# A SwiGLU FFN inside a two-block model: gate and up by seven half products, the FFN in two phases

## The chip, the cores and the metric

The kernel runs on one core of one Trainium2 chip. Its engines are TensorE (PE in the rows; PEld is its weight load), VectorE (DVE), ScalarE (ACT), GpSimd (POOL) and SyncE (SP), which here issues the DMAs. The metric is the device time of one execution in microseconds: 2137.47 us for the kernel before, the median of 3 runs (2134.62 to 2138.95).

## The reference

Two model blocks on 1024 tokens of width 1024, all in f32. The first has four mixers (mLSTM, a spatial gating unit, a convolution, S5), an output projection, a layer norm, and then the part that is changed here:

```python
x = layer_norm(ALPHA * x + g1 * y, ln1_w, ln1_b)
x = layer_norm(ALPHA * x + g2 * swiglu(x * (1.0 + sc2) + sh2, w_ffn_in, w_ffn_out), ln2_w, ln2_b)

def swiglu(h, w_in, w_out):
    g, u = split(h @ w_in, 2)            # w_in: 1024 x 5632
    return (silu(g) * u) @ w_out         # w_out: 2816 x 1024
```

The second block (retention, sparse attention, a gated embedding) starts on the result tile by tile.

## The kernel before

All data lie in pages of 128 x 1024 f32. Every f32 product is made of three matmuls of a fast f32 type: an operand is split into hi (ScalarE copies and rounds, L173) and lo (VectorE subtracts, L174), and hi x hi, lo x hi and hi x lo are added up in PSUM (L184 to L186, or L195 to L197 where the loop yields between them). A page pool (46 pages), a pool of 3 raw buffers for what is loaded and split, and PSUM in two pools of 4 banks (mm and ax) set when a load or a product may begin.

The FFN has 22 slices j of 128 of its 2816 columns. The layer-normed tokens, transposed, scaled and split (L334 to L341), lie in two halves of 512 tokens, hh and hl. For each slice and half, `Ffn.half` (L350) makes gate and up with 8 k x 3 matmuls of 512 columns each, then silu (ScalarE, L366), the product (VectorE, L367) and its split ah, al (L368, L369). `stage_b` (L372) goes over the slices in blocks of two: behind the four halves of a block it loads two slices of w_ffn_out, POOL multiplies them by the modulation row g2 (L412), they are split, and `item` (L429) makes the down product for each of the 8 token tiles, two column halves each, which VectorE adds to the tile's residual acc (L436). The last block's items go on to the second layer norm and into the second model block, in a pipe with that block's work.

The residual acc of the 8 tiles stays on chip from the first layer norm on. `residual` scales it in the first FFN block: two rows are scaled on POOL (L383), and each tile is multiplied (VectorE, L386) and added to (POOL, L387). Weights of the second model block are split beside the FFN and put by in DRAM ("spare", PS steps a block).

Each engine takes its instructions in the order in which the program records them, so the position of an operation in these loops sets what it is queued behind.

Of the kernel before, what the change touches and what calls it, by code (L numbers as in the profile page):

```python
# [255 lines left out]
class Front:  # L256


    def __init__(self, k, y_s, mod_s, x, wo, w_fi, have):
# [15 lines left out]
    def items(self):  # L275
# [9 lines left out]
        self.ffn = Ffn(self.k, self.hT, self.w_fi)  # L285
        yield self.ffn.half(0, 0, GS)

    def tile_in(self, t):
# [35 lines left out]
        s1, t1 = self.s1, self.t1
        for i in range(8):
# [4 lines left out]
            hi, lo = ph[0][:, i % 2], ph[1][:, i % 2]  # L330
            self.hT[t // 4].append((hi, lo))
            pt = k.ax.tile([128, 512], F32, name="ax")
            for j in range(4):
                nc.tensor.transpose(pt[:, j * 128:j * 128 + 128], self.acc[t // 4 * 4 + j][:, i * 128:i * 128 + 128], k.ident)  # L334
# [1 line left out]
            ht = page("htmp", shape=[128, 512])
            if i in HTA:
                nc.scalar.activation(ht, pt, AF.Identity, scale=s1[:, i:i + 1], bias=t1[:, i:i + 1])
            else:
                nc.vector.tensor_scalar(ht, pt, s1[:, i:i + 1], t1[:, i:i + 1], op0=ALU.mult, op1=ALU.add)  # L340
            (nc.vector if i % 2 else nc.gpsimd).tensor_tensor(lo, ht, hi, op=ALU.subtract)  # L341


class Ffn:


    def __init__(self, k, hT, w_fi):
        self.k, self.hT, self.w_fi, self.w, self.a = k, hT, w_fi, {}, {}

    def half(self, j, half, c=8):  # L350
        k, nc, page = self.k, self.k.nc, self.k.page
        if j not in self.w:
            self.w[j] = [k.wload(dap(self.w_fi, (i * (DFF // 128) + j) * 131072, [[1024, 128], [128, 8], [1, 128]]), [128, 8, 128])
                         for i in range(2)]
            self.a[j] = page("ah", dt=F32R), page("al", dt=F32R)
        (wg, wu), (ah, al) = self.w[j], self.a[j]
        hs = slice(half * 512, half * 512 + 512)
# [1998 lines left out]
```

## Time and profile before

| | |
|---|---|
| time, median of 3 runs | 2137.47 us (2134.62 to 2138.95) |
| profiled execution, its own time | 2141.31 us |
| its span, first to last instruction | 2139.5 us |
| mean granted TensorE clock | 0.971 of full speed |
| busy: TensorE, VectorE, ScalarE, POOL | 94%, 60%, 37%, 20% |
| FFN, first gate product to last down product | about 614 to 1340 us |
| HBM traffic over the span | 139 GB/s |

A row of a group of instructions has the line, the engine, the operation with output and inputs, the shape, the count, and then the busy time in us, the mean of one in ns, and the idle time just before them with what ended it. In a timeline a row starts with the start and the duration in us; the idle time before it stands in brackets. Matmuls overlap, so their pace is read from their starts.

### The profile page before, as it was taken

What the parts mean: (1) busy time and instruction counts of PE and PEld (TensorE: products, weight loads), DVE (VectorE), ACT (ScalarE), POOL (GpSimd) and SP (SyncE); (2) the same over time, 40 slices, a digit from 0 to 9 for tenths busy, and PEclk for the clock granted to TensorE, in tenths of its full rate; (3) what the DMA queues carried; (4) which work ended last, traced back from release to release, by engine and by line L of the source; (5) the groups of instructions that cost most, each with busy time, mean ns of one, the idle gap of its engine ahead of it and who ended that gap; (6) DMA issues with size and microseconds to landing.
All of it is one profiled execution on the core that took longest, in us unless ns stands there. A gap on an engine that the chain in (4) does not pass through costs nothing. (4 is left out here: it accounts for less than half of the span.)

```text
span 2139.5 us, 29059 instructions
## 1 busy us (share of the span) xinstructions
PE 2019.0 (94%) x10808; PEld 1673.6 (78%) x10808; DVE 1281.4 (60%) x2620; ACT 785.4 (37%) x1568; POOL 429.0 (20%) x465
## 2 busy tenths in 40 slices
PE   8897898999998999999999999899999998899998
PEld 3787897877877888888887788786787886688886
DVE  6967636476686334554446543857788746856533
ACT  2521134343131222222222221545787524355432
POOL 1454403112144000000000000441002221200032
PEclk9999898989999999999999999999999998999999
DMA  8465564456411335554345534313312205343611
GB/s 291 158 157 139 141 204 139 166 173 225 172 47 61 106 111 201 187 206 147 130 157 187 206 133 147 138 40 109 148 50 89 89 24 163 128 154 120 226 60 69
DMA packets 144334, 299.32 MB, mean 140 GB/s; under 512 B 30648, under 2 KB 70072, under 8 KB 144192
## 3 DMA queue, kind: packets, MB, share of 16 engines
q1 hardware_dynamic: 144192, 297.46, 41.5%
q8 instruction: 85, 1.39, 0.3%
q14 instruction: 57, 0.47, 0.1%
HBM read 208.81 MB, written 87.56 MB: 139 GB/s over the span
## 5 line engine op out<-in xcount | busy, mean ns | idle before, releaser
L195 PE MATMUL mm<-hh,whi 128*128 128x512 f32 x704 | 275.2, 391 | 4.4 <-ACT whi L173 4.4
L197 PE MATMUL mm<-hh,wlo 128*128 128x512 f32 x704 | 275.1, 391 | 1.4 <-DVE wlo L174 1.4
L196 PE MATMUL mm<-hl,whi 128*128 128x512 f32 x704 | 274.8, 390 | 0.0
L184 PE MATMUL mm<-whi,xTh 128*128 128x512 f32 (+1 forms) x576 | 227.8, 399 | 3.9 <-DMA whi<-scr_wsp 2.6
L185 PE MATMUL mm<-wlo,xTh 128*128 128x512 f32 (+1 forms) x576 | 225.2, 392 | 2.5 <-DMA wlo<-scr_wsp 2.5
L186 PE MATMUL mm<-whi,xTl 128*128 128x512 f32 (+1 forms) x576 | 223.7, 391 | 0.0
L174 DVE TENSOR_TENSOR wlo<-raw,whi 128x1024 fp32r<-128x1024 f32 (+2 forms) x99 | 126.0, 1293 | 129.4 <-ACT whi L173 128.7
L412 POOL TENSOR_TENSOR raw<-raw,g2b 128x1024 f32<-128x1024 f32 x22 | 54.1, 2463 | 597.2 <-DMA raw<-in_w_ffn_out 569.6
L195 PEld LDWEIGHTS mm<-hh,whi 128*128 128x128 f32 x704 | 132.5, 188 | 32.4 <-ACT whi L173 5.3
L197 PEld LDWEIGHTS mm<-hh,wlo 128*128 128x128 f32 x704 | 132.5, 188 | 30.0 <-DVE wlo L174 2.7
L184 PE MATMUL mm<-whi,hhi 128*128 128x256 f32 (+1 forms) x512 | 152.0, 297 | 3.3 <-DVE csg L1526 1.7
L196 PEld LDWEIGHTS mm<-hl,whi 128*128 128x128 f32 x704 | 132.6, 188 | 27.5
L186 PE MATMUL mm<-whi,hlo 128*128 128x256 f32 (+1 forms) x512 | 149.6, 293 | 1.9 <-POOL hlo L1370 1.5
L185 PE MATMUL mm<-wlo,hhi 128*128 128x256 f32 (+1 forms) x512 | 150.5, 294 | 0.0
L184 PE MATMUL ax<-whi,ah 128*128 128x512 f32 x352 | 139.1, 397 | 8.9 <-ACT whi L173 5.7
L173 ACT ACTIVATE whi<-raw 128x1024 fp32r<-128x1024 f32 (+2 forms) x99 | 100.9, 1047 | 125.7 <-DMA raw<-in_w_fi_o 68.3
L436 DVE TENSOR_TENSOR acc<-ax,acc 128x512 f32<-128x512 f32 x176 | 116.5, 684 | 41.0 <-PE ax L186 40.7
L185 PE MATMUL ax<-wlo,ah 128*128 128x512 f32 x352 | 138.8, 394 | 0.2 <-DVE wlo L174 0.2
L186 PE MATMUL ax<-whi,al 128*128 128x512 f32 x352 | 138.3, 393 | 0.0
L367 DVE TENSOR_TENSOR sg<-mm,sg 128x512 f32<-128x512 f32 x44 | 30.4, 690 | 168.0 <-PE mm L197 157.7
L184 PEld LDWEIGHTS mm<-whi,xTh 128*128 128x128 f32 x576 | 109.3, 190 | 26.4 <-DMA whi<-scr_wsp 4.5
L185 PEld LDWEIGHTS mm<-wlo,xTh 128*128 128x128 f32 x576 | 109.3, 190 | 22.5 <-DMA wlo<-scr_wsp 3.6
(616 smaller groups left out, 4477.6 us busy)
## 6 DMA issues: line engine op xcount, KB each, us to landing
raw<-in_w_fi_o SPq DMA_DIRECT2D x44, 512.0 KB
wmr<-in_w_mod SPq DMA_DIRECT2D x32, 512.0 KB
raw<-in_w_in_2o SPq DMA_DIRECT2D x24, 512.0 KB
scr_wsp<-phi SPq DMA_DIRECT2D x24, 512.0 KB
scr_wsp<-plo SPq DMA_DIRECT2D x24, 512.0 KB
whi<-scr_wsp SPq DMA_DIRECT2D x24, 512.0 KB
wlo<-scr_wsp SPq DMA_DIRECT2D x24, 512.0 KB
raw<-in_w_ffn_out SPq DMA_DIRECT2D x22, 512.0 KB
```

The lines of the kernel that those rows point to most:

```text
L173: nc.scalar.activation(hi, raw, AF.Copy)
L174: nc.vector.tensor_tensor(lo, raw, hi, op=ALU.subtract)
L184: nc.tensor.matmul(ps, ah, bh, start=k == 0, stop=False)
L185: nc.tensor.matmul(ps, ah, bl, start=False, stop=False)
L186: nc.tensor.matmul(ps, al, bh, start=False, stop=k == n - 1)
L195: nc.tensor.matmul(ps, ah, bh, start=k == 0, stop=False)
L196: nc.tensor.matmul(ps, ah, bl, start=False, stop=False)
L197: nc.tensor.matmul(ps, al, bh, start=False, stop=k == n - 1)
L367: nc.vector.tensor_tensor(sg, pu, sg, op=ALU.mult)
L412: nc.gpsimd.tensor_tensor(raw, raw, g2b, op=ALU.mult)
L436: nc.vector.tensor_tensor(v[:, cs], ps, v[:, cs], op=ALU.add)
```

## The change

Gate and up of one slice are together a product of a 2 x 2 block matrix of weights (gate and up by two halves of k) with a 2 x 2 block matrix of tokens (two halves of k by two halves of tokens). The change makes it with Strassen's scheme (seven block products and sums of blocks instead of eight products): each of the seven has 4 k x 3 matmuls of 512 columns, 84 a slice. The tokens' sums t1 to t4 are made once (`high_half`); each slice's sums of weights are made in `load`, four of them on POOL, and all seven operands are split; the sums of products are made on VectorE as the products leave PSUM (`one`, `two`, `three`, `four`).

The FFN then runs in two phases, since the token operands fill the pages: phase 1 makes the activations of all 22 slices and stores each to DRAM (`scr_act`); the residual is stored to DRAM too (`scr_res`), when it is made. Phase 2 is the down product, in a block of 2 and five of 4 slices: the activation is loaded again and split, w_ffn_out is multiplied and split as before, and the items of the first block load the residual, multiply it (VectorE) and add to it (POOL). The steps for the second model block's weights are dealt out anew over both phases.

```diff
+        nc.sync.dma_start(dap(self.res, t * 131072, [[1024, 128], [1, 1024]]), v)
...
+    def high_half(self):
+        k, nc, page, s1, t1, hf, B = self.k, self.k.nc, self.k.page, self.s1, self.t1, self.hf, self.B
+        fs = []
+        def split(n, i, x):
+            if i % 2 == 0:
+                self.sp = [page(f"{n}{c}{i}", F32R, [128, 2, 512]) for c in "hl"]
+            hi, lo = self.sp[0][:, i % 2], self.sp[1][:, i % 2]
+            nc.scalar.activation(hi, x, AF.Copy)
+            nc.vector.tensor_tensor(lo, x, hi, op=ALU.subtract)
+            B[n].append((hi, lo))
+        for i in range(4):
+            if i:
+                yield 1
+            f = page(f"hg{i}", shape=[128, 2, 512])
+            fs.append(f)
+            nc.vector.tensor_scalar(f[:, 0], self.turned(1, i), s1[:, i:i + 1], t1[:, i:i + 1], op0=ALU.mult, op1=ALU.add)
+            nc.scalar.activation(f[:, 1], self.turned(1, i + 4), AF.Identity, scale=s1[:, i + 4:i + 5], bias=t1[:, i + 4:i + 5])
+            nc.vector.tensor_tensor(hf[i], f[:, 0], hf[i], op=ALU.subtract)
+            split('t1', i, hf[i])
+        for i in range(4):
+            yield 1
+            nc.gpsimd.tensor_tensor(hf[i], fs[i][:, 1], hf[i], op=ALU.subtract)
+            split('t2', i, hf[i])
+        for i in range(4):
+            nc.gpsimd.tensor_tensor(hf[i + 4], hf[i + 4], hf[i], op=ALU.subtract)
+            split('t4', i, hf[i + 4])
+        for i in range(4):
+            yield 1
+            split('22', i, fs[i][:, 1])
+        for i in range(4):
+            yield 1
+            nc.gpsimd.tensor_tensor(fs[i][:, 0], fs[i][:, 1], fs[i][:, 0], op=ALU.subtract)
+            split('t3', i, fs[i][:, 0])
+        hf.clear()
...
+    def load(self, j):
+        k, nc = self.k, self.k.nc
+        raw = []
+        for i in range(2):
+            r = k.raw([128, 8, 128])
+            nc.sync.dma_start(r, dap(self.w_fi, (i * (DFF // 128) + j) * 131072, [[1024, 128], [128, 8], [1, 128]]))
+            raw.append(r)
+        (a11, a12), (a21, a22) = [(r[:, 0:4], r[:, 4:8]) for r in raw]
+        self.w[j] = w = {}
+        def split(n, x):
+            p = k.wpage("fw", shape=[128, 2, 4, 128])
+            k.split(p[:, 0], p[:, 1], x)
+            w[n] = p[:, 0], p[:, 1]
+        split('11', a11)
+        split('12', a12)
+        yield 1
+        sp = k.page("fsa", shape=[128, 2, 4, 128])
+        sq = k.page("fsb", shape=[128, 2, 4, 128])
+        nc.gpsimd.tensor_tensor(sp[:, 0], a21, a22, op=ALU.add)
+        nc.gpsimd.tensor_tensor(sp[:, 1], sp[:, 0], a11, op=ALU.subtract)
+        split('s1', sp[:, 0])
+        split('s2', sp[:, 1])
+        yield 1
+        nc.gpsimd.tensor_tensor(sq[:, 0], a12, sp[:, 1], op=ALU.subtract)
+        nc.gpsimd.tensor_tensor(sq[:, 1], a11, a21, op=ALU.subtract)
+        split('s4', sq[:, 0])
+        yield 1
+        split('s3', sq[:, 1])
+        split('22', a22)
...
+    def one(self, j):
+        k, nc = self.k, self.k.nc
+        self.o[j] = e, u = [k.page(n, shape=[128, 2, 512]) for n in ("fe", "fu")]
+        nc.scalar.activation(e[:, 1], self.prod(j, '11', '11', k.mm), AF.Copy)
+        yield 1
+        nc.vector.tensor_tensor(e[:, 0], self.prod(j, '12', '21', k.mm), e[:, 1], op=ALU.add)
+        nc.scalar.activation(e[:, 0], e[:, 0], AF.Silu)
+    def two(self, j):
+        k, nc = self.k, self.k.nc
+        e, u = self.o[j]
+        nc.vector.tensor_tensor(u[:, 0], self.prod(j, 's2', 't2', k.ax), e[:, 1], op=ALU.add)
+        yield 1
+        nc.vector.tensor_tensor(u[:, 1], self.prod(j, 's1', 't1', k.ax), u[:, 0], op=ALU.add)
+    def three(self, j):
+        k, nc = self.k, self.k.nc
+        e, u = self.o[j]
+        nc.vector.tensor_tensor(e[:, 1], self.prod(j, 's4', '22', k.ax), u[:, 1], op=ALU.add)
+        nc.scalar.activation(e[:, 1], e[:, 1], AF.Silu)
+        yield 1
+        ps = self.prod(j, 's3', 't3', k.ax)
+        nc.vector.tensor_tensor(u[:, 1], ps, u[:, 1], op=ALU.add)
+        nc.vector.tensor_tensor(u[:, 0], ps, u[:, 0], op=ALU.add)
+        nc.vector.tensor_tensor(e[:, 1], u[:, 1], e[:, 1], op=ALU.mult)
+    def four(self, j):
+        k, nc = self.k, self.k.nc
+        e, u = self.o.pop(j)
+        nc.vector.tensor_tensor(u[:, 0], self.prod(j, '22', 't4', k.mm), u[:, 0], op=ALU.add)
+        nc.vector.tensor_tensor(e[:, 0], u[:, 0], e[:, 0], op=ALU.mult)
+        nc.sync.dma_start(dap(self.act, j * 131072, [[1024, 128], [1, 1024]]), e.rearrange("p a b -> p (a b)"))
+        del self.w[j]
...
+    def rest(self):
+        n = DFF // 128
+        ld = self.ld[2]
+        for j in range(n):
+            for _ in self.two(j):
+                next(ld, None)
+            yield j
+            if j:
+                self.four(j - 1)
+            next(ld, None)
+            for _ in self.three(j):
+                next(ld, None)
+            for _ in ld:
+                pass
+            ld = self.load(j + 3) if j + 3 < n else iter(())
+            next(ld, None)
+            if j + 2 < n:
+                for _ in self.one(j + 2):
+                    pass
+        self.four(n - 1)
...
+    for j in front.ffn.rest():
+        if j >= 2:
+            for _ in range(1 + j % 2):
+                next(spare, None)
+    front.B.clear()
+    g2b, aw, ab = page("g2b"), page("aw"), page("ab")
+    k.bcast(g2b, mod_s, 5120, 1024)
+    for p, w in ((aw, ln1_w), (ab, ln1_b)):
+        k.bcast(p, w, 0, 1024)
+        nc.gpsimd.tensor_scalar(p, p, ALPHA, None, op0=ALU.mult)
+    blocks = [range(2)] + [range(j, j + 4) for j in range(2, NF, 4)]
+    for n, blk in enumerate(blocks):
+        last = n == len(blocks) - 1
+        acts, wf = [], []
+            acts.append(k.wload(dap(act, j * 131072, [[1024, 128], [1, 1024]]), [128, 1024]))
             raw = k.raw()
             nc.sync.dma_start(raw, dap(w_fo, j * 131072, [[1024, 128], [1, 1024]]))
             nc.gpsimd.tensor_tensor(raw, raw, g2b, op=ALU.mult)
             hl = page("whi", F32R), page("wlo", F32R)
             k.split(*hl, raw)
             wf.append(hl)
...
+            if n == 0:
+                acc[t] = page(f"acc{t}")
+                nc.sync.dma_start(acc[t], dap(res, t * 131072, [[1024, 128], [1, 1024]]))
+                nc.vector.tensor_tensor(acc[t], acc[t], aw, op=ALU.mult)
+                nc.gpsimd.tensor_tensor(acc[t], acc[t], ab, op=ALU.add)
```

On POOL at the start of the FFN there stood before the last subtractions of the token halves, the scaling of two rows, and eight residual additions, of which the first two are shown, ahead of the multiplication of w_ffn_out (numbers behind names are buffers):

```order
L341 TENSOR_TENSOR hl0_5860<-htmp_5867,hh0_5859 128x512
L341 TENSOR_TENSOR hl2_5892<-htmp_5899,hh2_5891 128x512
L341 TENSOR_TENSOR hl4_5925<-htmp_5932,hh4_5924 128x512
L341 TENSOR_TENSOR hl6_5957<-htmp_5964,hh6_5956 128x512
L383 TENSOR_SCALAR aw_5995<-aw_5995 128x1024
L383 TENSOR_SCALAR ab_5996<-ab_5996 128x1024
L387 TENSOR_TENSOR acc0_5499<-acc0_5499,ab_5996 128x1024
L387 TENSOR_TENSOR acc1_5316<-acc1_5316,ab_5996 128x1024
```

Now four subtractions (`L354`) are followed by 20 additions and subtractions of 512 columns. Shown are the last twelve: hg are tokens' sums t3, hf those of t2 (L382) and t4 (L385), fsa and fsb sums of weights:

```order
L382 TENSOR_TENSOR hf0_5736<-hg1_5919,hf0_5736 128x512
L385 TENSOR_TENSOR hf4_5821<-hf4_5821,hf0_5736 128x512
L392 TENSOR_TENSOR hg2_5972<-hg2_5972 128x512
L425 TENSOR_TENSOR fsa_6021<-raw_5777 128x512
L382 TENSOR_TENSOR hf2_5787<-hg2_5972,hf2_5787 128x512
L426 TENSOR_TENSOR fsa_6021<-fsa_6021,raw_5775 128x512
L385 TENSOR_TENSOR hf6_5853<-hf6_5853,hf2_5787 128x512
L430 TENSOR_TENSOR fsb_6022<-raw_5775,fsa_6021 128x512
L431 TENSOR_TENSOR fsb_6022<-raw_5775,raw_5777 128x512
L392 TENSOR_TENSOR hg3_6005<-hg3_6005 128x512
L382 TENSOR_TENSOR hf2_5787<-hg3_6005,hf2_5787 128x512
L385 TENSOR_TENSOR hf6_5853<-hf6_5853,hf2_5787 128x512
```

The residual's work has left this place; tokens' sums and weights' sums stand mixed, and the last one of t2 (`hf2_5787<-hg3_6005`) is the nineteenth of the twenty. On TensorE the first product behind the turned tiles is the one that reads t2:

```order
L335 MATMUL ax_6012<-ident_73,acc4_5031 128x128
L335 MATMUL ax_6012<-ident_73,acc5_5231 128x128
L335 MATMUL ax_6012<-ident_73,acc6_5409 128x128
L335 MATMUL ax_6012<-ident_73,acc7_5606 128x128
L184 MATMUL ax_6104<-t2h0_6043,fw_5942 128x512
L184 MATMUL ax_6128<-t1h0_5900,fw_5939 128x512
L185 MATMUL ax_6104<-t2l0_6044,fw_5942 128x512
L186 MATMUL ax_6104<-t2h0_6043,fw_5942 128x512
```

Every product stands behind this one on TensorE, where before the next products needed the token halves alone.

Where phase 1 now ends, SP's queue has this (before, the loads of a block stood among those of the next products' weights, with no store of an activation and no load of acc):

```order
L479 DMA scr_act_102<-fe_8920 128x1024
L155 DMA g2b_9290<-scr_mod_90 128x1024
L155 DMA aw_9291<-in_ln1_w 128x1024
L155 DMA ab_9292<-in_ln1_b 128x1024
L539 DMA raw_9304<-in_w_ffn_out 128x1024
L160 DMA raw_9311<-scr_act_102 128x1024
L479 DMA scr_act_102<-fe_9067 128x1024
L539 DMA raw_9317<-in_w_ffn_out 128x1024
L160 DMA raw_9484<-scr_act_102 128x1024
L539 DMA raw_9490<-in_w_ffn_out 128x1024
L563 DMA acc0_9324<-scr_res_103 128x1024
L563 DMA acc1_9344<-scr_res_103 128x1024
```

The store of the last activation (`fe_9067`) stands ahead of the second slice of w_ffn_out and of the eight loads of acc. POOL had at such a place only multiplications by g2b, four rows for two blocks after the last residual addition:

```order
L387 TENSOR_TENSOR acc7_5599<-acc7_5599,ab_5996 128x1024
L412 TENSOR_TENSOR raw_6198<-raw_6198,g2b_6196 128x1024
L412 TENSOR_TENSOR raw_6205<-raw_6205,g2b_6196 128x1024
L412 TENSOR_TENSOR raw_6588<-raw_6588,g2b_6196 128x1024
L412 TENSOR_TENSOR raw_6595<-raw_6595,g2b_6196 128x1024
```

Now it has there:

```order
L540 TENSOR_TENSOR raw_9490<-raw_9490,g2b_9290 128x1024
L565 TENSOR_TENSOR acc0_9324<-acc0_9324,ab_9292 128x1024
L565 TENSOR_TENSOR acc1_9344<-acc1_9344,ab_9292 128x1024
L565 TENSOR_TENSOR acc2_9364<-acc2_9364,ab_9292 128x1024
L565 TENSOR_TENSOR acc3_9384<-acc3_9384,ab_9292 128x1024
L565 TENSOR_TENSOR acc4_9404<-acc4_9404,ab_9292 128x1024
L565 TENSOR_TENSOR acc5_9424<-acc5_9424,ab_9292 128x1024
L565 TENSOR_TENSOR acc6_9444<-acc6_9444,ab_9292 128x1024
L565 TENSOR_TENSOR acc7_9464<-acc7_9464,ab_9292 128x1024
L540 TENSOR_TENSOR raw_9503<-raw_9503,g2b_9290 128x1024
L540 TENSOR_TENSOR raw_9516<-raw_9516,g2b_9290 128x1024
L540 TENSOR_TENSOR raw_9529<-raw_9529,g2b_9290 128x1024
```

The residual additions, eight in a row, have moved from the FFN's first block to this place, behind the first multiplication for block 1 and ahead of the other three.

## Rows read from the trace of the kernel before

**Rows 1.** The page: busy us, share of the span and instructions of each engine.

```profile
PE 2019.0 (94%) x10808; PEld 1673.6 (78%) x10808; DVE 1281.4 (60%) x2620; ACT 785.4 (37%) x1568; POOL 429.0 (20%) x465
```

**Rows 2.** The page's costliest group: busy us, mean ns, idle before.

```profile
L195 PE MATMUL mm<-hh,whi 128*128 128x512 f32 x704 | 275.2, 391 | 4.4 <-ACT whi L173 4.4
```

**Rows 3.** Timeline of TensorE: start, duration, in brackets the idle time before.

```profile
639.83 0.39 PE L196 MATMUL mm<-hl,whi 128*128 128x512 f32 x1
...
661.59 0.39 PE L196 MATMUL mm<-hl,whi 128*128 128x512 f32 x1
...
667.87 0.79 PE L184 MATMUL ax<-whi,ah 128*128 128x512 f32 x1 [5.67 <-ACT whi L173]
```

**Rows 4.** Windows: length, then busy of PE, PEld, DVE, ACT, POOL, clock, DMA, GB/s.

```profile
664.00:668.00 4.00, 0.13 (x1) 0.13 (x1) 0.15 (x1) 1.06 (x1) 4.00 (x3) 0.94 0.00 0
668.00:672.00 4.00, 3.77 (x8) 2.52 (x9) 4.00 (x4) 2.52 (x3) 1.04 (x1) 0.50 0.23 53
672.00:676.00 4.00, 4.00 (x14) 3.17 (x13) 2.90 (x5) 0.43 (x1) 0.00 (x0) 0.71 0.80 241
...
900.00:950.00 50.00, 50.00 (x222) 41.42 (x221) 24.84 (x32) 14.64 (x22) 3.21 (x2) 1.00 0.40 141
1150.00:1200.00 50.00, 46.10 (x195) 37.40 (x194) 21.67 (x30) 12.03 (x16) 4.79 (x2) 0.97 0.24 75
1200.00:1250.00 50.00, 48.41 (x212) 39.45 (x211) 26.09 (x31) 11.60 (x13) 4.80 (x2) 1.00 0.60 217
1350.00:1400.00 50.00, 43.92 (x202) 37.83 (x203) 34.73 (x88) 23.53 (x51) 21.16 (x31) 0.93 0.39 149
...
1380.00:1385.00 5.00, 2.39 (x7) 1.50 (x8) 2.90 (x19) 2.14 (x8) 2.05 (x7) 0.93 1.03 414
```

**Rows 5.** Timelines of VectorE (two rows), then of POOL.

```profile
618.81 0.81 DVE L320 TENSOR_SCALAR acc<-acc,rs_r,ln_nm 128x1024 f32<-128x1024 f32 x1
...
643.13 1.21 DVE L386 TENSOR_TENSOR acc<-acc,aw 128x1024 f32<-128x1024 f32 x1
...
621.87 3.00 POOL L341 TENSOR_TENSOR hl<-htmp,hh 128x512 fp32r<-128x512 f32 x2 [3.11 <-DVE htmp L340]
...
629.32 2.79 POOL L383 TENSOR_SCALAR aw<-aw 128x1024 f32<-128x1024 f32 x1
...
648.42 16.01 POOL L387 TENSOR_TENSOR acc<-acc,ab 128x1024 f32<-128x1024 f32 x5 [1.23 <-DVE acc L386]
664.40 4.65 POOL L412 TENSOR_TENSOR raw<-raw,g2b 128x1024 f32<-128x1024 f32 x2
...
716.34 2.39 POOL L412 TENSOR_TENSOR raw<-raw,g2b 128x1024 f32<-128x1024 f32 x1 [29.94 <-DMA raw<-in_w_ffn_out]
```

**Rows 6.** Line L341, one subtraction of 512 columns: ns min/median/max by engine.

```profile
L341 POOL TENSOR_TENSOR hl<-htmp,hh x8: 1282/1298/1974, 607.2 to 627.9; 128x512 fp32r<-128x512 f32 x8
L341 DVE TENSOR_TENSOR hl<-htmp,hh x8: 672/692/1483, 608.4 to 629.4; 128x512 fp32r<-128x512 f32 x8
```

**Rows 7.** Groups of the FFN's stretch: busy us, mean ns, idle before.

```profile
L436 DVE TENSOR_TENSOR acc<-ax,acc 128x512 f32<-128x512 f32 x164 | 108.5, 686 | 41.0 <-PE ax L186 40.7
L174 DVE TENSOR_TENSOR wlo<-raw,whi 128x1024 fp32r<-128x1024 f32 x68 | 85.8, 1290 | 120.4 <-ACT whi L173 120.1
L369 DVE TENSOR_TENSOR al<-sg,ah 128x512 fp32r<-128x512 f32 x44 | 46.8, 1063 | 26.2 <-ACT ah L368 26.2
L177 DVE SCALAR_TENSOR_TENSOR plo<-raw,cols,phi 128x512 fp32r<-128x512 f32 (+1 forms) x56 | 38.9, 736 | 4.5 <-ACT phi L176 4.4
...
L412 POOL TENSOR_TENSOR raw<-raw,g2b 128x1024 f32<-128x1024 f32 x22 | 54.1, 2463 | 597.2 <-DMA raw<-in_w_ffn_out 569.6 <-DVE sg L367 27.6
...
L368 ACT ACTIVATE ah<-sg 128x512 fp32r<-128x512 f32 x44 | 27.6, 628 | 173.2 <-DVE sg L367 173.2
```

**Rows 8.** Timelines of SP's DMA queue and of ScalarE at the next load.

```profile
670.15 3.59 SPq L160 DMA_DIRECT2D raw<-in_w_fi_o  x3
...
675.57 1.06 ACT L173 ACTIVATE whi<-raw 128x1024 fp32r<-128x1024 f32 x1 [3.97 <-DMA raw<-in_w_fi_o]
```

More of the change, by code (lines that the diff above doesn't have):

```diff
@@ L284, in items @@
             yield iter(())
-        self.ffn = Ffn(self.k, self.hT, self.w_fi)
-        yield self.ffn.half(0, 0, GS)
+        self.ffn = Ffn(self.k, self.B, self.w_fi, self.act)
+        yield self.ffn.first()
     def tile_in(self, t):
@@ L323, in tile_in, with turned, low_half @@
         yield from steps(WH0 if t == YT[-2] else WH1)
-        s1, t1 = self.s1, self.t1
+        if t == 0:
+            yield from self.low_half()
+        else:
+            yield from self.high_half()
+    def turned(self, half, i):
+        k, nc = self.k, self.k.nc
+        pt = k.ax.tile([128, 512], F32, name="ax")
+        for j in range(4):
+            nc.tensor.transpose(pt[:, j * 128:j * 128 + 128], self.acc[half * 4 + j][:, i * 128:i * 128 + 128], k.ident)
+        return pt
+    def low_half(self):
+        k, nc, page, s1, t1 = self.k, self.k.nc, self.k.page, self.s1, self.t1
         for i in range(8):
@@ L329, in tile_in @@
                 ph = [page(f"h{c}{i}", F32R, [128, 2, 512]) for c in "hl"]
[L330 to L334, printed above, removed]
+                hf = page(f"hf{i}", shape=[128, 2, 512])
+            hi, lo, f = ph[0][:, i % 2], ph[1][:, i % 2], hf[:, i % 2]
@@ L335, in tile_in @@
+            pt = self.turned(0, i)
             nc.scalar.activation(hi, pt, AF.Identity, scale=s1[:, i:i + 1], bias=t1[:, i:i + 1])
[L336 removed]
             if i in HTA:
[L338 removed]
+                nc.scalar.activation(f, pt, AF.Identity, scale=s1[:, i:i + 1], bias=t1[:, i:i + 1])
             else:
[L340 removed]
@@ L341, in tile_in @@
-            (nc.vector if i % 2 else nc.gpsimd).tensor_tensor(lo, ht, hi, op=ALU.subtract)
-class Ffn:
[L347 to L357, printed above, removed]
-        yield 1
-        while len(self.hT[half]) < 8:
-            yield 1
-        pg = k.mm.tile([128, 512], F32, name="mm")
-        yield from k.gemm_steps(pg, [((wg[0][:, i], wg[1][:, i]), self.hT[half][i]) for i in range(8)], c)
-        pu = k.mm.tile([128, 512], F32, name="mm")
-        yield from k.gemm_steps(pu, [((wu[0][:, i], wu[1][:, i]), self.hT[half][i]) for i in range(8)], c)
-        sg = page("sg", shape=[128, 512])
-        nc.scalar.activation(sg, pg, AF.Silu)
-        nc.vector.tensor_tensor(sg, pu, sg, op=ALU.mult)
-        nc.scalar.activation(ah[:, hs], sg, AF.Copy)
-        nc.vector.tensor_tensor(al[:, hs], sg, ah[:, hs], op=ALU.subtract)
@@ L415, in stage_b @@
             wf.append(hl)
-        if b0:
-            for _ in range(PS):
+        if n:
+            for _ in range(4):
                 next(spare, None)
-        if b0 == RT * FB:
+        if n == 3:
             early()
         if last:
+            for _ in spare:
+                pass
             w2c = k.col('ln2_w'), k.col('ln2_b')
@@ L2335, in pre @@
             c.begin()
-        stage_b(k, a.front.ffn, a.front.acc, S['mod'], I['ln1_w'], I['ln1_b'], I['w_ffn_out'],
+        stage_b(k, a.front, S['mod'], I['ln1_w'], I['ln1_b'], I['w_ffn_out'],
                 I['ln2_w'], I['ln2_b'], S['x2'], c.take, c.rot_tables, pre, c.rest, c.background, c.presplit())
```

68 lines of the change are left out of this document (31 added, 37 removed).

## The prediction, made before the run

> **What bounds the kernel now.** I read the page first: TensorE is busy for 94% of the span, the next engine (VectorE) for 60% [rows 1]. TensorE sets the time, but not by its busy column: the mean of an FFN matmul is 391 ns [rows 2], while in the timeline 97 of them start between 639.83 and 661.59 us, 96 steps of 21.76 / 96 = 0.2267 us, since they overlap [rows 3]. The windows then say where TensorE does not run at that pace: inside the FFN it works without a gap for most of the way (900 to 950 us: 50.00 of 50, clock 1.00), stands at 662 to 668, loses 3.9 us in 1150 to 1200 and 1.6 in 1200 to 1250, and 6.1 in 1350 to 1400, behind the FFN [rows 4]. So whatever takes matmuls out of the FFN is paid in full at 0.2267 us each, and whatever makes TensorE wait there costs in full as well.
>
> **The products: -59.8.** Before, a slice j has 96 gate and up matmuls (2 halves, gate and up, 8 k, 3 terms): 2112. Seven half products of 4 k and 3 terms are 84: 1848. 264 x 0.2267 = 59.8 us. By the busy mean it would be 103 us; the starts show that this is not to be had. The down product keeps its 1056 matmuls.
>
> **The FFN's start: +12.** Before, POOL had 8 subtractions of 512 columns there, the scaling of two rows, and 8 residual additions; these held up its first multiplication of w_ffn_out until 664.40 [rows 5], and TensorE, done with its products at 661.8, waited until 667.87 [rows 3] and then ran at granted clocks of 0.50 and 0.71 in two stretches of 4 us [rows 4]: 5.8 + 4 x 0.50 + 4 x 0.29, with some 0.6 of small waits 9.6 us. That stall goes, since the additions leave. What is late next is also POOL's: the order shows 4 subtractions, then 20 additions of 512 columns in a row, weights' sums mixed with tokens' sums, and product 4 of TensorE's order needs all four k of t2, whose last addition is the nineteenth. They can begin when tile 7 is normalised (618.81 + 0.81 [rows 5]) and turned: before, POOL's first operation behind that started at 621.87; now one VectorE subtraction and two splits (0.69 each) come first, so 623.3. A POOL operation of this size took 1.30 (median) to 1.48 us (mean of eight) [rows 6]: 19 of them end at 648 to 651.4; split and product take until 650 to 655. TensorE has four products (48 x 0.2267 = 10.9 us) and 32 transposes (4.5 us) from 613.65 on, and with the waits for the tile and for PSUM is through them at 632 to 635. So it idles for 16 to 19 us, and about 3 more go to the clock, as above: 21, less 9.6, is 12. Bounds: 5 (the additions at their minimum, the products later) and 20 (each at 1.7 us).
>
> **The body of phase 1: +3.** Two slices are 168 matmuls, 38.1 us. Beside them VectorE has 38 operations of 512 columns: 14 weight splits, 18 evictions, sums and products, 6 of the work put by for the second block. 24 of them read two operands in SBUF. At the rows' 0.68 to 0.74 us [rows 7] it is 26 us, and POOL has 8 x 1.30 = 10.4. Even if these excluded each other all the time, 36.4 are under 38.1. ScalarE has 14 splits and some 10 more operations of 0.63 [rows 7]: under 20 us. The weights come through three raw buffers; a load took 5.4 us from issue (670.15) to the split that waited for it (675.57) [rows 8], so two loads, four POOL additions and the splits of a slice are about 25 us of a chain with 38 to hide in. Traffic is some 7.5 MB in 38 us, 197 GB/s, and 414 has been moved in a stretch [rows 4]. So TensorE hides it, and I take 3 us for the margin being thin (0 to 20).
>
> **Between the phases: +30.** Here TensorE has nothing but phase 2, and phase 2 has to be fed from DRAM. T0 is the end of the last product. In SP's order the store of the last activation stands ahead of the load of w_ffn_out's second slice and all behind it; POOL has the two scalings (2.79 each [rows 5], begun before T0), three multiplications by g2b (2.46 each [rows 7]), then eight residual additions, and only then the three last slices of block 1. TensorE starts block 0 about T0 + 7 (the store and the reload of the last activation: a load's 5.4 and a split). Block 0 needs acc for its evictions, through four PSUM banks. Eight loads of 0.5 MB behind the others land from T0 + 14 on. Five residual pairs took 16.01 us on POOL, 3.20 each [rows 5], VectorE's half of each lying beside it: first pair done at 18.5, the eighth at 18.5 + 7 x 3.3 = 42. Then come three multiplications, and between them the raw buffers turn over (load 5.4, multiply 2.46, split 1.3, three buffers shared with the activations): 46, 52, 58. The order puts the fourth slice of block 1 last, so TensorE's first four groups of block 1 end at T0 + 58 to 61. Its own work up to there is 96 + 48 matmuls, 32.6 us. So 26 to 28 us are lost, and about 3 to the clock: 30 (18 to 45).
>
> The five pairs show 3.20 us, where a multiplication alone on VectorE (1.21) and an addition alone on POOL (2.39 is the time of a multiplication of that shape [rows 5]) would be 3.60 one behind the other. The Trainium skill, page "SBUF — State Buffer", section "Who interferes with whom", says that VectorE and GpSimd share a port pair as "an exclusive lock": an operation with two SBUF inputs shuts out the other engine's reads for the whole instruction. By that rule eight pairs would cost 8 x 0.4 = 3 us more, and the forecast would be 2120; the row decides for 3.20.
>
> **Phase 2 and its end: -6.** Blocks 2 to 5 have 192 matmuls, 43.5 us each, for eight loads, four multiplications and eight splits, a chain of 33 to 38 us by the durations above: hidden, +2 (0 to 10). VectorE adds to acc 96 times instead of 176, off the path. The last block now has four slices, 5.4 us of TensorE work a tile instead of 2.7, beside the start of the second model block, where 6.1 us are lost now: -5 (-10 to 0). The 5.5 us lost at 1150 to 1250 [rows 4] lie where the loads of the rotation tables stand among those of the weights; in the new order they have other neighbours: -3 (-6 to 0). The stores of the residual in front wait for a normalisation in SP's order and move later loads by under 2 us, beside 20 us of cover: 0 to 1, taken as 0.
>
> **Sum.** -59.8 + 12 + 3 + 30 + 2 - 5 - 3 = -20.8. The profiled execution's own time is 2141.31 us (span 2139.5), 3.8 above the median of 2137.47. 2141.3 - 20.8 = 2120.5 for a profiled execution, 2117 for the median.
>
> **Rivals.** (A) The two gaps are shorter: POOL's additions run near 1.28 and 2.71 us, because VectorE has little with two SBUF operands there, and the loads of acc land while the last products still run. Start +8, between the phases +18, body and phase 2 +1 each: -39.8, 2098. For it: the lone rows of POOL, 2.39 and 1.28. Against: VectorE splits beside every addition at the start.
>
> (B) The gaps eat the gain: start +18, between the phases +42 (the turn-over of three raw buffers goes at a load, a multiplication and a split each, with VectorE's splits queued behind its residual products), body +5: -0.8, 2137. For it: 16.01 us for five pairs shows how slow both engines get together. Against: it takes every step at its dear end.
>
> (C) The other side: VectorE becomes the bound of phase 1's body. Beside POOL a subtraction of 512 columns on VectorE took up to 1.48 us, and the splits of the activations average 1.06 against a median of 0.69 [rows 6, 7]. If all 24 operations with two SBUF operands took 1.48, a pair of slices would need 24 x 1.48 + 14 x 0.69 = 45.2 us, 7.1 over TensorE's 38.1: 11 pairs, +78, and 2195. It decides from 21 us on, 1.9 a pair, which is a mean of 1.26 us. Against: POOL works in 27% of the time there, so that a mean of 1.48 needs nearly each of them to meet it, and by exclusion alone a pair is 36.4 us. The skill's lock, named above, gives this same 36.4, so it does not make this case.
>
> **How the numbers follow.** The forecast's case 0.52 (its own range 2105 to 2130), A 0.20, B 0.13, C 0.15. A measurement of this kernel can tell 0.2%, 4.3 us: 2133.2 to 2141.7. Faster: 0.51 of the forecast's 0.52, all of A, a little of B (0.01): 0.72. Same: 0.01 and 0.08 of B: 0.09. Slower: C, and 0.04 of B: 0.19. The range reaches down past A to 2090 and up to 2148, where C's lower part and B's dear end lie; 0.06 below and 0.12 above are left out.
>
> **What would show it.** In the profile of the changed kernel: 1848 gate and up starts of 0.227 us apart through phase 1, some 420 us long with TensorE at 99%; a gap of TensorE of 15 to 20 us ending at 650 to 655, ended by ScalarE or VectorE splits of t2 behind POOL; a second one between the phases, ended by the splits of w_ffn_out and the evictions behind the residual additions, 26 to 28 us in all; clocks of 0.5 to 0.7 behind both. The prediction is wrong if TensorE's pace in the body is above 38.6 us a pair (C), or if the gap between the phases is under 20 or over 40 us.

## The result and the profile after

The changed kernel takes 2150.7 us (median of 8 runs, 2141.61 to 2157.89), the kernel before 2136.3 in the same series: a ratio of 1.0067 [1.0046, 1.0088], so 14 us slower where 21 less were forecast. Its profiled execution took 2157.89 us (span 2156.1), the slowest of the eight; it is compared by stages.

The engines' row of the page, the answer to [rows 1] (TensorE is busy for less of a longer span):

```profile
PE 1977.5 (92%) x10544; PEld 1634.7 (76%) x10544; DVE 1415.6 (66%) x2800; ACT 846.6 (39%) x1692; POOL 570.5 (26%) x561
```

What TensorE waited for from 590 to 1420 us (the operation that waits, then the one that it waits for; total us, times, longest):

```profile
PE ax L184 <- DVE acc L572: 25.5, 12, 5.6
PE ax L184 <- ACT t2h L367: 21.8, 1, 21.8
PE ax L184 <- ACT whi L173: 15.7, 4, 9.8
...
PE ax L185 <- DVE t2l L368: 2.7, 1, 2.7
```

One long wait for t2, and many for acc (an eviction of PSUM by VectorE that is late) and for operands of phase 2. Windows of the FFN, columns as in [rows 4]:

```profile
640.00:660.00 20.00, 2.69 (x6) 1.68 (x7) 17.02 (x16) 10.73 (x20) 16.90 (x11) 0.50 0.26 79
...
900.00:950.00 50.00, 50.00 (x222) 41.41 (x222) 36.99 (x51) 19.45 (x34) 16.23 (x11) 1.00 0.61 221
...
1050.00:1100.00 50.00, 33.54 (x120) 26.16 (x119) 25.97 (x29) 10.53 (x11) 19.59 (x8) 0.80 0.75 275
1100.00:1150.00 50.00, 41.31 (x146) 30.25 (x145) 38.23 (x34) 8.44 (x8) 21.70 (x9) 0.86 0.43 143
1150.00:1200.00 50.00, 46.26 (x192) 37.38 (x191) 29.59 (x29) 14.85 (x15) 11.92 (x5) 0.93 0.74 256
1200.00:1250.00 50.00, 49.18 (x216) 40.15 (x215) 30.30 (x32) 14.20 (x14) 11.00 (x4) 1.00 0.69 241
1250.00:1300.00 50.00, 42.02 (x171) 32.92 (x169) 35.32 (x43) 15.79 (x17) 18.20 (x7) 0.93 0.57 191
```

Phase 1's body stands as in [rows 4] before: no gap, clock 1.00, VectorE at 37 of 50. The time goes in three places: before it, behind it, and again at 1250.

A stage's loss is its length less 0.2267 us times the matmuls that started in it. Products 5 to 153 are 1787 matmuls, 405.1 us, and ran from 663.4 to 1068.6: no loss. From the first product to 700 us the start lost 35.0 us, and 14.0 before (the same 32 transposes are in both). From 1068.6 on, the first 71 us lost 39, the next 170 us 26 (waits and low clock together). To the last eviction the FFN lasts 774.9 us (614.4 to 1389.3), before 761.0 (613.6 to 1374.6); behind it 766.8 us follow, before 764.9.

| term | predicted | measured |
|---|---|---|
| products | -59.8 | -59.8 |
| FFN's start | +12 | +21 |
| body of phase 1 | +3 | 0 |
| between the phases (block 0, start of block 1) | +30 | +39 |
| later blocks of phase 2 | +2 | +26 |
| the end, and the 5.5 us of 1150 to 1250 | -8 | -12 (what remains) |
| FFN | -20.8 | +13.9 |

The start, in the timeline (start, us, line, operation; in brackets the wait ahead of it): TensorE's last operation on what it had, and its next product:

```profile
631.84 1.03 PE L335 MATMUL ax<-ident,acc 128*128 128x128 f32 x8
654.65 0.79 PE L184 MATMUL ax<-t2h,fw 128*128 128x512 f32 x1 [21.77 <-ACT t2h L367]
```

It stands for 21.77 us, as the waits above say, for the high part of t2. POOL's first and last operations on the way there:

```profile
625.14 1.28 POOL L392 TENSOR_TENSOR hg<-hg 128x512 f32<-128x512 f32 x1 [4.72 <-DVE hf L378]
626.39 1.73 POOL L425 TENSOR_TENSOR fsa<-raw 128x512 f32<-128x512 f32 x1
...
654.53 1.72 POOL L382 TENSOR_TENSOR hf<-hg,hf 128x512 f32<-128x512 f32 x1
```

And VectorE's splits at the end of it:

```profile
655.04 1.76 DVE L174 TENSOR_TENSOR fw<-raw,fw 128x512 fp32r<-128x512 f32 x1
656.72 3.56 DVE L368 TENSOR_TENSOR t2l<-hf,t2h 128x512 fp32r<-128x512 f32 x4
```

POOL's nineteen operations last from 625.14 to 656.25, 1.64 us each, where [rows 6] had 1.30 in the median; beside VectorE one takes 1.7, and VectorE's 1.75 instead of 0.69. Fifteen of the nineteen took 1.59 to 1.74 us, four 1.26 to 1.29.

Between the phases, POOL and VectorE at the residual:

```profile
1105.31 2.39 POOL L565 TENSOR_TENSOR acc<-acc,ab 128x1024 f32<-128x1024 f32 x1 [1.23 <-DVE acc L564]
1108.86 2.39 POOL L565 TENSOR_TENSOR acc<-acc,ab 128x1024 f32<-128x1024 f32 x1 [1.16 <-DVE acc L564]
1112.47 2.40 POOL L565 TENSOR_TENSOR acc<-acc,ab 128x1024 f32<-128x1024 f32 x1 [1.23 <-DVE acc L564]
1116.10 2.39 POOL L565 TENSOR_TENSOR acc<-acc,ab 128x1024 f32<-128x1024 f32 x1 [1.23 <-DVE acc L564]
1123.34 2.53 POOL L540 TENSOR_TENSOR raw<-raw,g2b 128x1024 f32<-128x1024 f32 x1 [4.85 <-DMA raw<-in_w_ffn_out]
```

The pairs start 3.55 to 3.63 us apart: addition (2.39) and multiplication (1.2) one behind the other. The next multiplication by g2b then waits 4.85 us for its load.

SP's queue around the first activation's load of blocks 2, 3 and 4 (start, us, line, transfer):

```profile
1148.62 0.77 SPq L160 DMA_DIRECT2D raw<-scr_act  x1
...
1188.80 0.45 SPq L160 DMA_DIRECT2D raw<-in_w_ple_gate  x1
1189.31 0.67 SPq L160 DMA_DIRECT2D raw<-scr_act  x1
...
1233.59 0.85 SPq L160 DMA_DIRECT2D raw<-in_w_ple_gate  x1
1234.49 1.14 SPq L160 DMA_DIRECT2D raw<-scr_act  x1
```

Rounds of 41 and 45 us, against 43.5 us of matmuls in a block. Each of the two holds twelve loads through the raw buffers, the block's eight and four spare ones (`in_w_ple_gate` is one of these), and the last goes out less than 1 us before the next block's first: the loads fill the round from end to end. How a late load reaches TensorE is seen in the next round:

```profile
1265.16 3.84 POOL L540 TENSOR_TENSOR raw<-raw,g2b 128x1024 f32<-128x1024 f32 x1 [6.05 <-DMA raw<-in_w_ffn_out]
...
1270.12 1.23 DVE L174 TENSOR_TENSOR wlo<-raw,whi 128x1024 fp32r<-128x1024 f32 x1 [3.36 <-ACT whi L173]
...
1272.20 0.69 DVE L572 TENSOR_TENSOR acc<-ax,acc 128x512 f32<-128x512 f32 x1
...
1272.94 0.80 PE L184 MATMUL ax<-whi 128*128 128x512 f32 x1 [4.32 <-DVE acc L572]
```

POOL multiplies the late load until 1269.00, VectorE waits 3.36 us for its high part, the eviction is queued behind that split, and TensorE waits 4.32 us for the eviction.

### The profile page after: what moved, and what is told of

Read it like the earlier page. It is cut to its first block, busy times and chain, and to the rows that moved or that the text cites. A ratio compares the mean times of both kernels' runs of the same rounds, so it can differ in the third digit from the quotient of the medians.

```text
span 2156.1 us, 29392 instructions
## 1 busy us (share of the span) xinstructions
PE 1977.5 (92%) x10544; PEld 1634.7 (76%) x10544; DVE 1415.6 (66%) x2800; ACT 846.6 (39%) x1692; POOL 570.5 (26%) x561
## 5 line engine op out<-in xcount | busy, mean ns | idle before, releaser
L184 PE MATMUL mm<-whi,xTh 128*128 128x512 f32 (+1 forms) x576 | 228.4, 400 | 4.0 <-DMA whi<-scr_wsp 2.8
L184 PE MATMUL ax<-whi 128*128 128x512 f32 x352 | 145.9, 421 | 41.3 <-DVE acc L572 25.5
L184 PE MATMUL mm<-whi,hhi 128*128 128x256 f32 (+1 forms) x512 | 152.0, 297 | 1.8 <-ACT zd L1603 0.9
L185 PE MATMUL ax<-wlo,whi 128*128 128x512 f32 x352 | 145.2, 413 | 2.8 <-DVE wlo L174 2.7
L186 PE MATMUL ax<-whi,wlo 128*128 128x512 f32 x352 | 144.6, 411 | 0.0
L184 PEld LDWEIGHTS mm<-whi,xTh 128*128 128x128 f32 x576 | 109.3, 190 | 25.9 <-DMA whi<-scr_wsp 4.1
L186 PEld LDWEIGHTS mm<-whi,xTl 128*128 128x128 f32 x576 | 109.4, 190 | 21.1 <-DVE xTl L801 0.6
L184 PEld LDWEIGHTS ax<-whi 128*128 128x128 f32 x352 | 70.8, 203 | 64.5 <-DVE acc L572 29.3
L904 ACT ACTIVATE junk<-score,candf 128x384 bf16<-128x384 f32 (+1 forms) x124 | 96.1, 775 | 34.5 <-DVE candf L925 31.9
L184 PEld LDWEIGHTS mm<-whi,hhi 128*128 128x128 f32 x512 | 100.9, 197 | 4.1 <-ACT zd L1603 1.3
L186 PEld LDWEIGHTS mm<-whi,hlo 128*128 128x128 f32 x512 | 100.8, 197 | 3.1 <-POOL hlo L1505 1.9
L185 PEld LDWEIGHTS mm<-wlo,hhi 128*128 128x128 f32 x512 | 101.0, 197 | 0.7 <-issue 0.6
L572 DVE TENSOR_TENSOR acc<-ax,acc 128x512 f32<-128x512 f32 x96 | 64.2, 683 | 45.9 <-PE ax L186 40.4
```

What stands on the lines that cost most here:

```text
L184: nc.tensor.matmul(ps, ah, bh, start=k == 0, stop=False)
L185: nc.tensor.matmul(ps, ah, bl, start=False, stop=False)
L186: nc.tensor.matmul(ps, al, bh, start=False, stop=k == n - 1)
L572: nc.vector.tensor_tensor(v[:, cs], ps, v[:, cs], op=ALU.add)
L904: nc.scalar.activation(junk[:, :w], x, AF.Sign, scale=-1.0, bias=c, accum_out=cnt[:, j:j + 1])
```

## The experiments

The theory: the start is the making of t2 by VectorE and POOL; between the phases the residual pairs; in the later blocks the three raw buffers, through which 8 loads and up to 4 spare ones a block have to pass. Times are medians of 4 to 12 executions; ratios are to the kernel before, differences to the changed kernel's 2150.7 where nothing else is said. Profiled executions reached the FFN at 602 to 615 us, also where the code ahead of it is the same (all but e2 and e5), so stages are compared by length: phase 1 from the first matmul to the last start on L184 of the last product but one, phase 2 from there to the start of the last eviction. Losses are reckoned as above.

| run | time us | ratio, 95% | phase 1 | phase 2 |
|---|---|---|---|---|
| changed kernel | 2150.7 | 1.0067 [1.0046, 1.0088] | 450.7 | 324.2 |
| e1 | 2146.2 | 1.0048 [1.0029, 1.0067] | 448.2 | 324.6 |
| e2 | 2138.0 | 1.0017 [1.0001, 1.0034] | 457.4 | 298.8 |
| e3 | 2194.7 | 1.0287 [1.0266, 1.0308] | 506.3 | 324.8 |
| e4 | 2120.1 | 0.9935 [0.9918, 0.9952] | 450.7 | 295.9 |
| e5 | 2117.4 | 0.9923 [0.9906, 0.9941] | 455.8 | 277.7 |
| e6 | 2120.8 | 0.9926 [0.9906, 0.9945] | 448.6 | 296.6 |
| e7 | 2126.9 | 0.9953 [0.9936, 0.9969] | 450.0 | 302.9 |
| e8 | 2128.1 | 0.9972 [0.9959, 0.9986] | 449.7 | 302.4 |
| e9 | 2120.0 | 0.9936 [0.9917, 0.9955] | 464.4 | 278.5 |
| e10 | 2115.7 | 0.9919 [0.9888, 0.9950] | 456.2 | 284.4 |
| e11 | 2088.9 | 0.9790 [0.9766, 0.9815] | 436.4 | 279.4 |
| e12 | 2117.0 | 0.9923 [0.9903, 0.9943] | 457.3 | 284.8 |

### e1: less on POOL at the start

```diff
-            nc.gpsimd.tensor_tensor(hf[i + 4], hf[i + 4], hf[i], op=ALU.subtract)
...
+                nc.vector.tensor_tensor(hf[i + 4], hf[i + 4], hf[i], op=ALU.subtract)
...
-            nc.gpsimd.tensor_tensor(fs[i][:, 0], fs[i][:, 1], fs[i][:, 0], op=ALU.subtract)
...
+                nc.vector.tensor_tensor(fs[i][:, 0], fs[i][:, 1], fs[i][:, 0], op=ALU.subtract)
...
-        ld = self.ld[2]
+        ld = chain(self.ld[1], self.ld[2])
```

> Of the tokens' sums, t3 and t4 go from POOL to VectorE, behind t2, and the sums of weights of the second slice come behind the first product that needs t2, so that POOL has 8 operations before t2's last instead of 19. Theory (the first gap is POOL's queue, 1.68 us an operation): t2 is split some 14 us sooner, about 646 instead of 660, and the time falls from the changed kernel's 2150.7 to 2137 (2133 to 2141). Rival (VectorE, which shares the work and has the splits of the weights in the same stretch, is late by itself): t2 is split no sooner than 655, and the time stays at 2146 to 2151.

4.5 us less. The time is the rival's, the split of t2 lies between the two. Not shown in the code: the splits of 22, t3 and t4 move behind the first product with t2. TensorE's largest waits to 700 us:

```profile
PE ax L184 <- ACT t2h L367: 8.4, 2, 7.7
PE ax L185 <- DVE 22l L368: 4.4, 1, 4.4
...
PE ax L185 <- DVE t2l L368: 2.7, 2, 1.6
```

The last part of t2 was split at 649.5 instead of 660.3 (37 us behind the first product instead of 46), but then the operand 22 was late (4.4), since VectorE had the sums of t4 ahead of its split, and phase 1 was 2.5 us shorter in all. POOL's queue alone was not the cause.

### e2: the residual scaled in front

```diff
-        nc.sync.dma_start(dap(self.res, t * 131072, [[1024, 128], [1, 1024]]), v)
+        rs = page("rs")
+        nc.vector.tensor_tensor(rs, v, self.aw, op=ALU.mult)
+        nc.gpsimd.tensor_tensor(rs, rs, self.ab, op=ALU.add)
+        nc.sync.dma_start(dap(self.res, t * 131072, [[1024, 128], [1, 1024]]), rs)
...
-                nc.vector.tensor_tensor(acc[t], acc[t], aw, op=ALU.mult)
-                nc.gpsimd.tensor_tensor(acc[t], acc[t], ab, op=ALU.add)
```

> The residual is multiplied and added to when each tile leaves the first layer norm, into a page of its own, and put by in DRAM scaled; the items of phase 2's first block only load it. Theory (eight residual pairs on VectorE and POOL hold the evictions and the last multiplications of block 1): the loss between the phases, 39 us from the last product to 1140, falls to some 20, and the time from 2150.7 to 2132 (2128 to 2137). Rival (the loads and splits through three raw buffers hold TensorE there, and the pairs lie beside them): under 8 us, 2143 or more. If the front has no room for 16 operations and three pages, it loses there what the boundary gains.

12.7 us less. The first 71 us behind phase 1 lose 16 instead of 39, as the theory has it; the later blocks lose 24 as ever. Phase 1 is 6.7 longer, and at 600 us, just ahead of the FFN, there is a wait of 6.0 us for macc (part of the modulation, summed on VectorE) that the changed kernel does not have there:

```profile
PE ax L1472 <- DVE macc L1464: 6.0, 1, 6.0
PE ax L342 <- DVE hf L360: 2.9, 1, 2.9
PE mm L185 <- POOL hl L361: 2.7, 1, 2.7
```

The two smaller waits lie at the start of phase 1. The last 700 matmuls and transposes ahead of the FFN take 152.4 us, in all runs without the pairs there 141.4 to 144.7. So the front had no cover for the pairs: of the 25.4 us gained in phase 2 about half is given back by the time, by the trace 6.7 in phase 1 and some 10 in front.

### e3: the second block's weights all in phase 1

```diff
-            for _ in range(1 + j % 2):
+            for _ in range(2 + (j % 5 == 1)):
...
-        if n:
-            for _ in range(4):
-                next(spare, None)
```

> All 44 steps for the second block's weights in phase 1 (two a slice, three in every fifth), none in phase 2: there 14 loads, splits and 28 stores fewer. Theory (the later blocks lose because three raw buffers turn over too slowly for 8 loads and up to 4 spare ones a block): the 25 us lost from 1140 to 1310 fall to some 12, the time to 2138 (2133 to 2143). Rival (the later blocks lose to VectorE's and POOL's slow pairs and to the rotation tables at 1250 to 1262): 4 us at most, 2146 to 2151. If phase 1's cover is used up by the added steps, the time is above 2151.

44 us more: a case that the expectation names last, and far dearer. The waits of TensorE:

```profile
PE mm L184 <- ACT fw L173: 41.4, 12, 10.1
PE ax L184 <- ACT whi L173: 27.4, 3, 22.3
```

Phase 1 is 56 us longer, with weights (fw) that came late; one wait of 22.3 us lies at the boundary, where the last spare loads stood ahead of phase 2's and the changed kernel waited 9.8. The blocks from 121 to 241 us behind phase 1 lost 7 instead of 18: with eight loads a block, not twelve, three buffers nearly do. Which resource phase 1 ran out of was left to e8.

### e4: the activations past the raw buffers

```diff
-            acts.append(k.wload(dap(act, j * 131072, [[1024, 128], [1, 1024]]), [128, 1024]))
+            ar = page("ar")
+            nc.sync.dma_start(ar, dap(act, j * 131072, [[1024, 128], [1, 1024]]))
+            ahl = page("ah", F32R), page("al", F32R)
+            k.split(*ahl, ar)
+            acts.append(ahl)
```

> In phase 2 the activations are loaded into pages instead of raw buffers, which leaves the three raw buffers to w_ffn_out and the spare weights: half of the loads go past them. Theory (turn-over of three raw buffers): the loss from 1140 to 1310 falls by 12 to 15 us, and 3 to 6 go between the phases, to 2134 (2129 to 2140). Rival (the pairs and the tables): 4 us at most, 2146 to 2151.

30.6 us less, more than expected. The boundary loses 33 instead of 39, the later blocks 4 instead of 26. Windows of e4:

```profile
1150.00:1200.00 50.00, 50.00 (x222) 41.40 (x221) 38.26 (x35) 14.25 (x14) 15.76 (x5) 1.00 0.66 243
1200.00:1250.00 50.00, 48.48 (x212) 39.16 (x210) 36.90 (x45) 13.94 (x15) 11.79 (x4) 1.00 0.60 215
1250.00:1300.00 50.00, 48.42 (x212) 39.82 (x213) 32.43 (x33) 11.85 (x12) 12.28 (x5) 1.00 0.64 231
```

VectorE and POOL have the same work, VectorE busier in two of the three windows; so the slow pairs and the rotation tables alone were not what the later blocks lost to. The tables have a part in it where the buffers leave no slack: in the changed kernel 17 of the 26 us lie from 1250 to 1310, with the tables at 1248 to 1272, while e4, with the tables at 1225 to 1238, loses 4 from 1180 to 1300.

### e5: e2 and e4 together

> Both edits together: the residual scaled in front and loaded only, and the activations loaded into pages. Theory (two separate causes: residual pairs between the phases, 23 us of the 39 lost there; raw buffers in the later blocks, 22 of 25): the gains add up, less the 7 us that the front lost, so 2120 - 23 + 7 = 2104 (2098 to 2112). Rival (both edits relieve the same wait, the raw chain of block 1): 2114 or more.

The time is the rival's, its mechanism is not: most of the two gains add up, phase 2 is 277.7, 46.5 shorter (28.3 and 25.4 alone). But the time is only 2.7 us below e4's: phase 1 is 5.1 longer, the wait for macc in front is there again (5.3 us), and the last 700 operations of TensorE ahead of the FFN take 152.1 us, in e4 141.6. With phase 2 18.2 shorter than e4's these sum to 2.6. Two causes, as the theory says, and the same price in front.

### e6: the start in another order, with e4

```diff
         next(self.ld[0])
         next(self.ld[1])
+        for _ in self.ld[0]:
+            pass
         yield 1
...
+                nc.vector.tensor_tensor(fs[i][:, 0], fs[i][:, 1], fs[i][:, 0], op=ALU.subtract)
...
-        ld = self.ld[2]
+        ld = chain(self.ld[1], self.ld[2])
```

> Activations through pages, and the start in another order: all of slice 0's weights are summed and split before tile 7 is normalised, slice 1's and t4's splits come behind product 4, t3 is summed on VectorE. Before t2's last sum POOL has seven operations, VectorE 21 from the first turned tile. Theory (VectorE and POOL together are what t2 waits for, so taking work out of the stretch counts, not moving it from one to the other): t2 is split at about 30 us from the first product instead of 46, of which some 4 go to tile 7's own delay: 12 us, 2108 (2102 to 2114). Rival (as in the first experiment, what is saved at t2 comes back at the next operands): 3 us, 2117.

No gain (2120.8 against e4's 2120.1). t2 is split 39 us behind the first product, where the theory had 30 instead of 46. The start's waits are now in many places:

```profile
PE ax L184 <- ACT t2h L367: 5.0, 2, 4.1
PE ax L335 <- ACT hf L351: 4.5, 1, 4.5
PE ax L185 <- DVE t2l L368: 3.7, 3, 2.5
...
```

The rival holds: what is saved at t2 comes back at the next operands.

### e7 and e8: four raw buffers

e7 is one line; e8 adds e3's edit.

```diff
-NQ = 46
-NR = 3
+NQ = 45
+NR = 4
```

> The changed kernel with four raw buffers instead of three and 45 pages instead of 46, nothing else. Theory (three raw buffers turn over too slowly in phase 2): the later blocks lose under 10 us instead of 25, the boundary some 5 less, 2131 (2122 to 2140). Rival (the pages helped since loads no longer stood behind each other in the raw order, a fourth buffer is not enough): 2145 or more. If 45 pages hold up phase 1, its TensorE share falls below 99% and the time is above 2151.

> Four raw buffers and 45 pages, and all 44 steps for the second block's weights in phase 1. With three raw buffers this lost 56 us in phase 1, with 41 us of waits for weight splits. Theory (raw buffers bound phase 1 too as soon as 4.2 loads a slice go through three of them): 35 us or more of these come back, 2160 or less. Rival (VectorE, POOL and the traffic are full with these steps): the waits stay, 2180 or more.

23.8 us less in e7, and e8 takes back 67 us of e3's: its phase 1 is 449.7 instead of 506.3, and no wait for fw, the weights of phase 1, is left (whi is phase 2's):

```profile
PE ax L184 <- ACT t2h L367: 22.9, 1, 22.9
PE ax L184 <- ACT whi L173: 17.2, 3, 14.7
```

One buffer more, and neither VectorE, POOL nor the traffic held phase 1 up: what e3 had run out of is raw buffers. In phase 2 the four runs part the loss from 121 to 241 us behind phase 1:

| | three buffers | four buffers |
|---|---|---|
| with the spare loads | 18 (changed kernel) | 11 (e7) |
| without them | 7 (e3) | 0 (e8) |

In this stretch the spare loads make 11 of the 18 us, the missing buffer 7. Dealt out early they cost as much elsewhere: in the 121 us before, e3 and e8 lose 59 and 44 where the changed kernel and e7 lose 47 and 33, and phase 2 is no shorter without them. e7's theory was missed in size: its later blocks lose 12 from 71 us on, not under 10, and 11 of these lie in the 60 us that end with the rotation tables.

### e9, e10 and e12: the residual inside phase 1

```diff
...
+        if 4 <= j < 20 and j % 2 == 0:
+            at = dap(res, (j // 2 - 2) * 131072, [[1024, 128], [1, 1024]])
+            rs = page("rs")
+            nc.sync.dma_start(rs, at)
+            nc.vector.tensor_tensor(rs, rs, aw, op=ALU.mult)
+            nc.gpsimd.tensor_tensor(rs, rs, ab, op=ALU.add)
+            nc.sync.dma_start(at, rs)
...
```

> Activations through pages, and the residual scaled inside phase 1: at eight slices a tile is loaded, multiplied, added to and stored again, in a page; phase 2 only loads it. Theory (the residual pairs cost 23 us between the phases; in front they found no cover, in phase 1 they lie beside TensorE's products): 2120 - 23 = 2097, with phase 1 no longer than before (2092 to 2104). Rival (phase 1's cover is used up too, as when all spare steps were put there): phase 1 grows by 10 us or more, 2107 or more.

> The same with four raw buffers and 45 pages. Theory (with the activations in pages the raw buffers are relieved already; what is left between the phases is the round trip of the last activation and the loads of w_ffn_out): 4 us less than with three, some 2093. Rival (the raw turn-over still bounds block 1): 10 us less, 2087.

> Pages, residual in phase 1, four raw buffers, and the start's other order (slice 0's weights early, slice 1's and t4's splits late, t3 on VectorE). Theory (the start is bound by VectorE and POOL together, so order moves little): 2 to 4 us less than without the other order, about 2090. Rival (with a fourth raw buffer the late weights of slices 1 and 2 no longer come back as waits): 10 us less, 2083.

e9 is where its rival put it: phase 2 is 17 us shorter than e4's, phase 1 13.7 longer, with waits for weight splits (7.2 us) that e4 has not. In e10 the fourth raw buffer gives 8 us back in phase 1 and loses 6 in phase 2. Its 2115.7 is the lowest median with all the sums made, 0.8% below the kernel before, but its interval holds the ratios of e4, e5, e6, e9 and e12: none of these is shown to be faster than e4. e12's order again brings nothing.

### e11: the tokens' sums left out, on e9

```diff
...
-            nc.vector.tensor_tensor(hf[i], f[:, 0], hf[i], op=ALU.subtract)
-            split('t1', i, hf[i])
...
+            split('22', i, f[:, 1])
+        B['t1'], B['t2'], B['t3'], B['t4'] = list(B['11']), list(B['21']), list(B['11']), list(B['21'])
```

> The kernel of e9 without the tokens' sums: t1 to t4 are not made, the products read the operands of the low half in their place (the output is another one); 12 sums, 16 splits and four of eight turned blocks fall away at the start. Theory (the first gap is the making of these operands on VectorE, POOL and ScalarE): TensorE waits under 5 us in all at the start, and the time is 18 to 22 below e9's. Rival (the sums and splits of the weights of the first slices make the gap): 8 us below at most.

31 us below e9, more than either side expected (it leaves out 16 sums, not 12: twelve on POOL and four on VectorE). No wait for a token sum is left in phase 1. TensorE waits 4.7 us in all to 700 us; the largest of phase 1:

```profile
PE ax L335 <- DVE acc L320: 3.5, 1, 3.5
PE ax L184 <- DVE fu L455: 1.9, 4, 0.8
...
PE mm L184 <- ACT fw L173: 1.2, 2, 0.7
```

Phase 1 is 28.0 us shorter. Its first 60 us lose 9.6 instead of e9's 35.2, which is 25.6 of the 28 (the 16 transposes that are left out too, at 0.11 us, make some 2 of these); the rest of the phase loses 11.2 instead of 13.7. So the first gap is the making of t1 to t4. Without them 16 pages are free as well; the runs do not tell how much of the 2.5 us of the rest is theirs.

## Why the prediction was wrong

The products and the body of phase 1 came as forecast: 0.2267 us a matmul, and VectorE, three quarters busy, did not become the bound (rival C falls). The sign was lost in three terms.

**Later blocks of phase 2, +2, measured +26.** This is the step that failed: "eight loads, four multiplications and eight splits, a chain of 33 to 38 us by the durations above: hidden". Two things are missing in it. The list leaves out the spare loads, up to four a block, which pass through the same three buffers: in the trace a round has twelve loads. And the chain is summed from durations, as if each buffer were free as soon as its engines could have been done; but each operation queues on its engine behind others, in order, and the eviction behind a late split waits with it. In the trace the loads fill the whole round, 41 and 45 us, where TensorE needs 43.5. There was no margin, and delays went on to TensorE. Without the spare loads (e3) the blocks from 121 us on lost 7 instead of 18; with half of a block's own loads past the buffers (e4) 22 of the 26 us were gone; with a fourth buffer (e7) 14 of them, and phase 2 was 21 shorter. How much of the rest the rotation tables make is open.

**Between the phases, +30, measured +39.** Mechanism right: without the pairs (e2) the stretch lost 16. The size fell short by the pair, 3.6 us instead of 3.20 to 3.3, and by the loads: SP issued the fourth slice of block 1 only at 1129, so that it was multiplied at 1133.7, T0 + 65 instead of 58. The Trainium skill, page "SBUF — State Buffer", section "Who interferes with whom", says that a VectorE instruction with two SBUF inputs contends with a GpSimd one that reads SBUF, and calls their shared port pair "an exclusive lock"; the pairs here, 2.39 + 1.2 = 3.6 us, agree with it. The forecast had taken the 3.20 of the kernel before against it, and that was a misreading. The 16.01 us are four steps from one addition to the next, 3.31 us each on average, and a last addition beside which VectorE had no multiplication. And VectorE's row beside them, which was not read, shows the same exclusion:

```profile
644.87 14.55 DVE L386 TENSOR_TENSOR acc<-acc,aw 128x1024 f32<-128x1024 f32 x5
```

Five multiplications took 14.55 us there, where one alone took 1.21 [rows 5].

**The start, +12, measured +21.** The place and the operand (t2, the nineteenth operation of POOL) were right. The operation was taken at 1.30 to 1.48 us; nineteen of them took 1.64, since fifteen ran long beside VectorE's operations, which is near the bound that the forecast gave (+20 at 1.7 us each). They also began at 625.1 instead of 623.3, and the splits of t2 lay behind one of the weights. That POOL's queue was the cause held only in part: e1 and e6 took operations off it and moved the wait to VectorE; e11 took the work away, and the wait went.

Of the rivals B was nearest, 2137 with gap terms of 18 and 42; they were 21 and 39, the same 60 in sum, but B too held the later blocks to be hidden (+2), where they lost 26, and it gave 5 us to the body of phase 1, which lost none.

## What to carry to other kernels

For a pool of few buffers, count every load that passes through it, also those of other work, and add up how long each really holds its buffer, queues of all engines that it passes included; then hold the round against the time of the block. The chain summed here at 76 to 87% of it was not hidden. Where VectorE and GpSimd both work on two operands in SBUF, sum their durations, do not take the longer: pairs of 2.39 and 1.21 us came 3.31 to 3.63 us apart. Work that is moved out of one stage has to find cover in the next: the same residual cost 23 us between the phases, some 16 in front and at the start of phase 1 (10 and 5 to 7), 14 inside phase 1.
